# The up projection of a ConvFFN: sums of weight blocks formed by accumulating DMA transfers

## The chip, the cores and the metric

The kernel runs on one core of a Trainium2 chip. The metric is the device time of one execution in microseconds (us); lower is better. Three runs of the kernel before gave 2246.61, 2250.70 and 2250.82 us, with a median of 2250.7. The engines are TensorE (PE, matrix products), VectorE (DVE), ScalarE (ACT), GpSimd (POOL) and SyncE (SP, which here only issues DMA transfers). A core has 16 DMA engines, which queues of the issuing engines feed.

## The reference, cut to what matters

The model has two layers, 1024 tokens (`T`) and a width of 1024. Each layer mixes tokens first and then adds a ConvFFN. Only the ConvFFN is touched here, and it is computed twice, once for each layer:

```
def conv_ffn(h, w_up, conv_w, conv_b, w_down):      # h: 1024 x 1024, w_up: 1024 x 5632
    a, b = jnp.split(h @ w_up, 2, axis=-1)          # each 1024 x 2816
    a_pad = jnp.pad(a, ((0, 0), (CONV_WIDTH - 1, 0), (0, 0)))
    a = sum(a_pad[:, j:j + T] * conv_w[j] for j in range(CONV_WIDTH)) + conv_b   # CONV_WIDTH = 3
    return (jax.nn.silu(a) * b) @ w_down            # w_down: 2816 x 1024
...
x = x + conv_ffn(rmsnorm(x, g_ffn[l]), w_up[l], conv_w[l], conv_b[l], w_down[l])
```

All of it is float32. PE multiplies in a rounded form of it (fp32r), so every operand is split into a rounded upper part `hi` and the remainder `lo`, and one product is three matrix multiplications: hi·hi, hi·lo and lo·hi.

## The kernel before, in words

**Tiling of the up projection.** The products are blocked 2 x 2: the inner dimension of 1024 in two halves, the tokens in two halves of 512, and the two outputs `a` and `b`. The 2816 columns of each output are cut in 22 pieces of 128. One piece is a unit (class `Up`), with four weight blocks A11, A12 (of `a`, first and second half of the inner dimension) and A21, A22 (of `b`). A block is 128 partitions by 512 float32 numbers, 256 KB. A scheme of the Strassen and Winograd kind gives the four output blocks from seven block products instead of eight. The left operands of products 1, 2 and 4 are the loaded blocks A11, A12 and A22; those of products 6, 7, 3 and 5 are sums of the blocks. The right operands are made from the normalised tokens once per layer (`blocks1`, L575 and behind), for all units.

**One unit.** A product (`product`, L1053, matmuls at L1058 to L1060) is 12 matmuls of 128 x 512: four slices of 128 by three multiplications. PE runs the products of a unit in the order 1, 6, 2, 7, 5, 4, 3, adding into three banks: `fx` (products 1 and 2), `fy` (6, 7 and 4) and `fw` (5 and 3). Between them DVE adds results up: `q` (L1092) is product 6 plus `s1`, the copy of product 1 that ACT makes at L1082; `t` (L1097) is formed after product 7, which is added into the same bank as product 6. PE may start product 7 only when DVE has read the bank for `q`. Behind these come the three taps of the convolution (ACT L1117, DVE L1119 and L1123), Silu on ACT (L1138), the products with `b` on DVE (L1107, L1143), and sums of neighbouring units (L1147, `mixed`), which are stored to memory for the down projection (SP, L1170).

**The weights of a unit.** SP loads the four blocks (`load`, L1019) into two tiles of 128 x 1024. `direct` splits A11 (key 1) and the pair A12, A22 (keys 2 and 4): ACT rounds the upper part (L1022) and DVE subtracts it (L1023). Then `sums` (L1042 to L1045) overwrites the blocks in the same two tiles with the four sums, by four tensor_tensor operations, on DVE for the first four units of a layer and on POOL for the other 18:

```
(a0, b0), (a1, b1) = ((t[:, hs(0)], t[:, hs(1)]) for t in self.raw)
tt = (nc.vector if self.soon else nc.gpsimd).tensor_tensor
tt(b1, b0, b1, ALU.add)          # L1042
tt(b0, a0, b0, ALU.subtract)     # L1043
tt(a0, b1, a0, ALU.subtract)     # L1044
tt(a1, a1, a0, ALU.subtract)     # L1045
```

`split67` and `split35` then split two sums each, as one operation of 1024 columns on ACT and one on DVE.

**The order.** The first two units (the pair) run side by side while the right operands are still made. Products 1 and 2 of the next four units (`pre`) are computed in that stage as well, stored, and read back later (`again`, L1075 and L1076); these units are called early here. After the pair, units are run one behind another (`run`), a unit and an early one by turns, and then the remaining twelve. The program names two orders by hand: `follow(..., "order")` puts a split behind a given instruction on ACT and on DVE, and `mix` does so for the sums of neighbours. Everything else is put in order by a scheduler, engine by engine; on its engine each instruction then runs in order. In the profiled execution the up projection of layer 0 lies at about 412 to 841 us and that of layer 1 at about 1595 to 2025 us; the down projections follow.

Of the kernel before, what the change touches and what calls it, by code (L numbers as in the profile page):

```python
# [14 lines left out]
P = 128  # L15
# [4 lines left out]
NF = 22  # L20
# [14 lines left out]
def kernel(  # L35
# [543 lines left out]
    def blocks1(norm, gc, B):  # L579
        rs = norm.done()  # L580
        yield "norm"
        lo, hi = xs[:4], xs[4:]
        a, b = hs(0), hs(1)
        tt = nc.vector.tensor_tensor

        for r in (7, 6, 5, 4, 3):
            B[r] = []
        for j in range(4):
            scaled_x(1, rs, gc, (j, 4 + j))
            nc.sync.dma_start(h_d[j], hi[j][:, b])  # L590
            tt(lo[j][:, b], hi[j][:, b], lo[j][:, b], ALU.subtract)
            tt(lo[j][:, a], lo[j][:, b], lo[j][:, a], ALU.add)
            B[6].append(rl(lo[j][:, a], s="B"))
        for j in range(4):
            B[7].append(rl(lo[j][:, b], s="B"))
        yield "67"
        for j in range(4):
            tt(lo[j][:, b], hi[j][:, b], lo[j][:, a], ALU.subtract)
# [380 lines left out]
    def ffn(l, blocks_, after):  # L979
# [8 lines left out]
        def slot(what, n, make):  # L988
            if what not in ring:
                ring[what] = [make() for _ in range(n)]  # L990
                turn[what] = 0
            turn[what] += 1
            return ring[what][turn[what] % n]

        turn = {}

        def either(n):
            if "A" not in ring:
                ring["A"] = [(V(F32R, "Ah"), V(F32R, "Al")) for _ in range(2)]
            return ring["A"][n]  # L1000

        def raws():
            return [wp.tile([P, 1024], F32, tag="raw", name=nm("wu"), bufs=4) for _ in range(2)]

        class Up:
# [5 lines left out]
            def load(self, k=None):  # L1011
                if k is None:
                    self.load(0)
                    k = 1
                if k == 0:
                    self.raw = slot("raw", 2, raws)
                t = self.raw[k]
                for j in (1, 0) if self.early else (0, 1):
                    nc.sync.dma_start(t[:, hs(j)], w_up[l, j * NF + self.i, :, hs(k)])  # L1019
# [9 lines left out]

            def direct(self):  # L1030
                t = slot("one", 2, lambda: wrl("A"))
                hi, lo = t[:, hs(0)], t[:, hs(1)]
                if self.early:
                    self.split((4,), self.raw[1][:, hs(1)], hi, lo)
                else:
                    self.split((1,), self.raw[0][:, hs(0)], hi, lo)
                    self.split((2, 4), self.raw[1], *slot("two", 2, lambda: (wrl("Ah"), wrl("Al"))))

            def sums(self):
                (a0, b0), (a1, b1) = ((t[:, hs(0)], t[:, hs(1)]) for t in self.raw)  # L1040
                tt = (nc.vector if self.soon else nc.gpsimd).tensor_tensor
                tt(b1, b0, b1, ALU.add)  # L1042
                tt(b0, a0, b0, ALU.subtract)  # L1043
                tt(a0, b1, a0, ALU.subtract)  # L1044
                tt(a1, a1, a0, ALU.subtract)  # L1045
# [142 lines left out]
        def ahead(then, after):  # L1188
            if after is not None:
                after.load(1)  # L1190
            if then is not None and then.early:
                then.again()

        def run(u, last, then, after):
            nxt = [then] if then is not None else []
            if u.s1 is None:
                u.p1()
            u.p6()
            if after is not None:
                after.load(0)  # L1200
            if u.early:
# [3 lines left out]
                u.split35((then.kept, u.opened))  # L1205
                ahead(then, after)
                u.p7()
                u.taps0()
            else:
                u.p2()  # L1210
                each(last[:1], "end")
                u.split35((u.kept, u.opened))
                ahead(then, after)
# [15 lines left out]
            mix(u.ended)  # L1229
            u.p3()  # L1230
# [8 lines left out]
        for n, u in enumerate(seq):  # L1239
            u.n, u.mate = n // 2, seq[n - 1] if n % 2 else None  # L1240
            u.soon = n < 4
        each(pair, "load", "direct")
# [4 lines left out]
        each(pair, "sums")  # L1247
# [3 lines left out]
        each(pair, "split67", "p6", "p7")  # L1251
        next(rest)
        each(pair, "act0", "split35", "p5")
# [6 lines left out]
        then.sums()  # L1260
        each(pair, "p3")
        then.split67()
# [112 lines left out]
        def add_x(ps, k, half):  # L1375
            xv = xs[k][:, hs(half)]
            tt(xv, ps, xv, ALU.add)
# [40 lines left out]
        def down():  # L1418
# [40 lines left out]
            for t0, w in segs_:  # L1459
                c = slice(t0, t0 + w)  # L1460
                for m in range(4):
# [3 lines left out]
                    tt(xv, bank[m][:, c], xv, ALU.add)  # L1465
# [557 lines left out]
```

## Time and profile before

| | |
|---|---|
| median of three runs | 2250.7 us |
| the profiled execution | 2249.9 us |
| its span | 2248.1 us |
| mean granted TensorE clock | 0.997 |
| PE busy | 2207.3 us, 98% of the span |
| DVE busy | 1723.6 us, 77% |
| ACT busy | 1116.3 us, 50% |
| POOL busy | 420.0 us, 19% |
| queue q1 (SP's transfers) | 263.11 MB, 35.4% of the 16 DMA engines |
| queue q0 (POOL's transfers) | 11.65 MB, 1.5% |

The span is the stretch that the hardware profiler recorded; the execution's own time has 1.8 us more. Busy shares are means over the whole span. What holds PE up in one stage is seen only where the trace is cut into stretches of time, and in the waits: an entry such as `[1.75 <-DVE q L1092]` behind an instruction says that its engine stood idle for 1.75 us before it and that DVE's instruction of line 1092, which writes `q`, released it. In a row of a stretch, each engine has its busy time and its number of instructions, followed by the granted clock, the busy share of the DMA engines and the GB/s.

### The profile page before, as it was taken

The page shows a single profiled execution, that of the slowest core. Times are in us where ns is not written, and L with a number is a line of the kernel's source. Part 1 is how long each engine was busy: PE and PEld are TensorE (multiplying, and loading weights), DVE is VectorE, ACT ScalarE, POOL GpSimd, SP SyncE. Part 2 cuts the span into 40 slices and gives each one's busy share as a digit, 9 for nine tenths or more (in the row PEclk, how much of TensorE's full clock was granted, in tenths as well). Part 3 has the DMA queues.
Part 4 walks back from the last instruction along what each step waited for, and adds up shares of the span by engine and source line. Part 5 has one row for each costly group of instructions (what it writes and reads, how often), then busy time and mean ns, then how long its engine had stood idle before and what let it go on. Part 6 is the DMA issues. An engine that isn't in the chain of part 4 may idle for free.

```text
span 2248.1 us, 32203 instructions
## 1 busy us (share of the span) xinstructions
PE 2207.3 (98%) x11522; PEld 1839.3 (82%) x11522; DVE 1723.6 (77%) x3037; ACT 1116.3 (50%) x2085; POOL 420.0 (19%) x409
## 2 busy tenths in 40 slices
PE   9999999999999999999999999999999999999998
PEld 7888887777888888888888888888778888888886
DVE  6886886887877768887756778866987877768877
ACT  6564464543333335456545688874543333335445
POOL 1312210013332210000103323320013322210000
PEclk9999999999999999999999999999999999999999
DMA  6332246334332329544421111036434333329533
GB/s 228 103 104 87 79 156 215 132 127 134 129 122 99 108 78 353 169 136 141 129 85 42 48 48 36 9 116 212 138 127 132 127 122 103 106 74 349 164 94 112
DMA packets 138942, 285.20 MB, mean 127 GB/s; under 512 B 15709, under 2 KB 22446, under 8 KB 138782
## 3 DMA queue, kind: packets, MB, share of 16 engines
q1 hardware_dynamic: 130430, 263.11, 35.4%
q0 software_dynamic: 3600, 11.65, 1.5%
q10 hardware_dynamic: 4752, 8.39, 1.0%
q8 instruction: 90, 1.47, 0.3%
q14 instruction: 70, 0.57, 0.1%
HBM read 211.27 MB, written 71.83 MB: 126 GB/s over the span
## 4 chain that ended last, share of the span: by engine, by line
PE 79%; DVE 11%; ACT 4%; DMA 3%; issue 2%; SPq 0%; POOL 0%; DVEq 0%; ACTq 0%; POOLq 0%
PE dn L1413 6%; PE dn L1414 6%; PE dn L1412 6%; PE fy L1058 5%; PE fy L1060 5%; PE fy L1059 5%; PE fx L1058 3%; PE fx L1059 3%; PE fx L1060 3%; PE fw L1060 3%; PE fw L1058 3%; PE fw L1059 3%; PE op L195 2%; PE op L196 2%; PE op L194 2%
## 5 line engine op out<-in xcount | busy, mean ns | idle before, releaser
L1412 PE MATMUL dn<-db,da 128*128 128x512 f32 (+1 forms) x628 | 242.5, 386 | 0.0
L1413 PE MATMUL dn<-db,da 128*128 128x512 f32 (+1 forms) x628 | 242.1, 386 | 0.3 <-DVE db L1342 0.3
L1414 PE MATMUL dn<-db,da 128*128 128x512 f32 (+1 forms) x628 | 241.6, 385 | 0.0
L1058 PE MATMUL fy<-B,Ah 128*128 128x512 f32 x496 | 195.4, 394 | 8.5 <-DVE q L1092 7.3
L1060 PE MATMUL fy<-B,Al 128*128 128x512 f32 x496 | 194.0, 391 | 0.4 <-DVE Al L1023 0.4
L1059 PE MATMUL fy<-B,Ah 128*128 128x512 f32 x496 | 193.8, 391 | 0.0
L1042 POOL TENSOR_TENSOR wu<-wu,wu 128x512 f32<-128x512 f32 x36 | 47.2, 1311 | 730.7 <-DVE Al L1023 568.5
L1022 ACT ACTIVATE Ah<-wu 128x1024 fp32r<-128x1024 f32 x124 | 130.4, 1052 | 102.9 <-PE fy L1059 60.3
L1023 DVE TENSOR_TENSOR Al<-wu,Ah 128x1024 fp32r<-128x1024 f32 x124 | 160.8, 1298 | 8.5 <-ACT Ah L1022 7.4
L1413 PEld LDWEIGHTS dn<-db,da 128*128 128x128 f32 x628 | 117.9, 188 | 25.6 <-DVE db L1342 1.8
L1412 PEld LDWEIGHTS dn<-db,da 128*128 128x128 f32 x628 | 118.0, 188 | 24.1 <-issue 0.2
L1060 PE MATMUL fw<-B,Al 128*128 128x512 f32 x352 | 137.7, 391 | 0.0
L1059 PE MATMUL fw<-B,Ah 128*128 128x512 f32 x352 | 137.0, 389 | 0.0
L1058 PE MATMUL fw<-B,Ah 128*128 128x512 f32 x352 | 137.0, 389 | 0.0
L1414 PEld LDWEIGHTS dn<-db,da 128*128 128x128 f32 x628 | 117.9, 188 | 23.2
L1342 DVE TENSOR_TENSOR db<-bl,db 128x512 fp32r<-128x512 f32 x154 | 105.8, 687 | 27.9 <-ACT db L1341 27.3
L1058 PEld LDWEIGHTS fy<-B,Ah 128*128 128x128 f32 x496 | 93.5, 188 | 33.7 <-DVE q L1092 12.3
L1341 ACT ACTIVATE db<-bl 128x512 fp32r<-128x512 f32 x154 | 95.7, 621 | 34.0 <-PE dn L1414 26.4
L1060 PEld LDWEIGHTS fy<-B,Al 128*128 128x128 f32 x496 | 93.5, 189 | 20.9 <-DVE Al L1023 1.1
L1059 PEld LDWEIGHTS fy<-B,Ah 128*128 128x128 f32 x496 | 93.5, 188 | 19.0
L1138 ACT ACTIVATE fc<-fc 128x512 f32<-128x512 f32 x88 | 54.9, 626 | 106.3 <-DVE fc L1119 85.3
L1341 ACT ACTIVATE da<-wb 128x512 fp32r<-128x512 f32 x88 | 55.1, 629 | 99.4 <-PE dn L1413 67.4
(415 smaller groups left out, 6152.2 us busy)
## 6 DMA issues: line engine op xcount, KB each, us to landing
wu<-in_w_up_dram SPq DMA_DIRECT2D x176, 256.0 KB, 3.0
bl<-gb_d SPq DMA_DIRECT2D x154, 256.0 KB, 2.8
gb_d<-fc SPq DMA_DIRECT2D x132, 256.0 KB, 2.5
wb<-in_w_down_dram SPq DMA_DIRECT2D x44, 256.0 KB, 3.9
wa<-in_w_down_dram SPq DMA_DIRECT2D x22, 512.0 KB, 7.8
wo<-in_a_wo_dram SPq DMA_DIRECT2D x16, 512.0 KB, 3.8
xre<-om_d SPq DMA_DIRECT2D x32, 256.0 KB, 4.2
x_r<-x SPq DMA_DIRECT2D x32, 256.0 KB, 2.4
```

What stands on the lines that cost most here:

```text
L1022: a = nc.scalar.activation(hi, src, AF.Copy)
L1023: b = nc.vector.tensor_tensor(lo, src, f(hi), ALU.subtract)
L1042: tt(b1, b0, b1, ALU.add)
L1058: mm(ps, wr, hr, start=(first and j == 0), stop=False, skip_group_check=True)
L1059: mm(ps, wr, hl, start=False, stop=False, skip_group_check=True)
L1060: mm(ps, wl, hr, start=False, stop=(stop and j == 3), skip_group_check=True)
L1138: silu[0] = nc.scalar.activation(self.c[half], self.c[half], AF.Silu)
L1341: nc.scalar.activation(w[:, hs(0)], t, AF.Copy)
L1342: b = tt(w[:, hs(1)], t, f(w)[:, hs(0)], ALU.subtract)
L1412: mm(o, hi, bh, start=first, stop=False, skip_group_check=True)
L1413: mm(o, hi, bl, start=False, stop=False, skip_group_check=True)
L1414: mm(o, lo, bh, start=False, stop=stop or n == NP - 1, skip_group_check=True)
```

## The change

**Where the sums are made.** The four sums of a unit are no longer made by DVE or POOL. SP loads A11 and A22 into one tile `R`, A12 into a half tile `Q` and A11 once more into a half tile `T`. POOL then issues DMA transfers that read a weight block from memory and add it to what stands in the target (`more`, with `accum_op=ALU.add`): T += A21 and T += A22 give the sum for product 6; R += A21 on both halves gives those for products 7 and 5 (after `direct` has split A11 and A22 from the same tile); T += A12 gives that for product 3 (after product 6's sum was split). These are five accumulating transfers of 256 KB per unit, 110 per layer. The left operand of product 3 is thus formed in the same place as that of product 6, from it.

**Splits.** The keys split together change: (1, 4) as one operation of 1024 columns, 2 alone, (7, 5) together, 6 alone, 3 alone. `split3` is placed by hand behind product 5's sum (`u.summed`) on DVE and behind Silu on ACT. The splits go to tiles named by what is dead there (`area`), six of one kind and four of another, instead of rings of two; the four raw tiles are now R0, R1 (by turns), Q and T (a half for each parity of the unit).

**Signs.** An accumulating transfer can only add here, so some sums come out with another sign. On the right side three kinds of sum (one addition and two subtractions) become a scalar_tensor_tensor that computes -p - q in place of a tensor_tensor (`neg_sub`, 12 per layer), and in the down projection the result is subtracted from x instead of added.

The core of the diff:

```diff
@@ blocks1
+        def neg_sub(o, p, q):
+            nc.vector.scalar_tensor_tensor(o, p, -1.0, q, ALU.mult, ALU.subtract)
+
...
-            tt(lo[j][:, a], lo[j][:, b], lo[j][:, a], ALU.add)
+            neg_sub(lo[j][:, a], lo[j][:, b], lo[j][:, a])
...
-            tt(lo[j][:, b], hi[j][:, b], lo[j][:, a], ALU.subtract)
-            tt(hi[j][:, a], hi[j][:, a], lo[j][:, a], ALU.subtract)
+            neg_sub(lo[j][:, b], hi[j][:, b], lo[j][:, a])
+            neg_sub(hi[j][:, a], lo[j][:, a], hi[j][:, a])
@@ class Up
+            def load(self):
+                self.load_r()
+                self.load_q()
+                self.sum_t(0)
+                self.sum_t(1)
+
+            def load_r(self):
+                self.place()
+                nc.sync.dma_start(self.R[:, hs(0)], self.block(0, 0))
+                nc.sync.dma_start(self.R[:, hs(1)], self.block(1, 1))
+
+            def load_q(self):
+                if not self.early:
+                    nc.sync.dma_start(self.Q, self.block(0, 1))
+                nc.sync.dma_start(self.T, self.block(0, 0))
+
+            def more(self, t, j, k):
+                nc.gpsimd.dma_start(t, self.block(j, k), accum_op=ALU.add)
+
+            def sum_t(self, k):
+                self.more(self.T, 1, k)
+
+            def sum_r(self):
+                for h in range(2):
+                    self.more(self.R[:, hs(h)], 1, 0)
+
+            def sum_s4(self):
+                self.more(self.T, 0, 1)
...
-            def sums(self):
-                (a0, b0), (a1, b1) = ((t[:, hs(0)], t[:, hs(1)]) for t in self.raw)
-                tt = (nc.vector if self.soon else nc.gpsimd).tensor_tensor
-                tt(b1, b0, b1, ALU.add)
-                tt(b0, a0, b0, ALU.subtract)
-                tt(a0, b1, a0, ALU.subtract)
-                tt(a1, a1, a0, ALU.subtract)
-
-            def split67(self, past=None):
-                self.split((6, 7), self.raw[0], *either(self.i == 1), past)
-
-            def split35(self, past=None):
-                self.split((3, 5), self.raw[1], *either(self.i != 0), past)
+                    self.split((1, 4), self.R, hi, lo)
+                    self.one(2, self.Q, "Z3" if self.pos == 1 else "Z2")
+
+            def split75(self, past=None):
+                hi, lo = (area(k) for k in (("Z2", "Z3") if self.pos == 1 else ("Y0", "Y1")))
+                self.split((7, 5), self.R, hi, lo, past)
+
+            def split6(self, past=None):
+                self.one(6, self.T, "Z7" if self.pos % 2 else "Z6", past)
+
+            def split3(self, past=None):
+                self.one(3, self.T, ("Z6", "Z7")[self.pos] if self.pos < 2 else "Z3", past)
@@ run(u, last, then, after)
             u.act0()
-            each(nxt, "sums")
+            each(nxt, "sum_r")
             u.p5()
             mix(u.summed)
+            u.split3((u.acted, u.summed))
+            each(two, "load_q")
             for v in nxt:
-                v.split67((u.acted, u.drained))
+                v.split6((u.acted, u.drained))
+                v.sum_s4()
+            for v in two:
+                v.sum_t(0)
+                v.sum_t(1)
...
             u.p4()
             mix(u.ended)
+            each(nxt, "split75")
             u.p3()
@@ the tail of the down projection (and add_x alike)
-                    tt(xv, bank[m][:, c], xv, ALU.add)
+                    tt(xv, xv, bank[m][:, c], ALU.subtract)
```

**How it moves POOL's instructions.** The first place is on POOL, among the late units of layer 0 (`wu_639` to `wu_642` are the four raw tiles; after the change 639 and 642 are R0 and R1, 640 is Q and 641 is T). Before, for two units:

```order
L1042 TENSOR_TENSOR wu_640_3520<-wu_639_3519,wu_640_3520 128x512
L1043 TENSOR_TENSOR wu_639_3519<-wu_639_3519 128x512
L1044 TENSOR_TENSOR wu_639_3519<-wu_640_3520,wu_639_3519 128x512
L1045 TENSOR_TENSOR wu_640_3520<-wu_640_3520,wu_639_3519 128x512
L1042 TENSOR_TENSOR wu_642_3522<-wu_641_3521,wu_642_3522 128x512
L1043 TENSOR_TENSOR wu_641_3521<-wu_641_3521 128x512
L1044 TENSOR_TENSOR wu_641_3521<-wu_642_3522,wu_641_3521 128x512
L1045 TENSOR_TENSOR wu_642_3522<-wu_642_3522,wu_641_3521 128x512
```

Now, for two units:

```order
L1038 DMA wu_639_3519<-in_w_up_dram 128x512 x2
L1038 DMA wu_641_3521<-in_w_up_dram 128x512
L1038 DMA wu_642_3528<-in_w_up_dram 128x512
L1038 DMA wu_641_3521<-in_w_up_dram 128x512
L1038 DMA wu_642_3528<-in_w_up_dram 128x512
L1038 DMA wu_641_3521<-in_w_up_dram 128x512 x4
```

Eight tensor operations became ten issues of transfers, of which those on R and on T stand in one in-order queue, one behind another.

**How it moves DVE's instructions.** The second place is on DVE ahead of `q` of the third unit behind the pair, in layer 0 (the wait of PE at 520 us before). `Ah` and `A` are halves of splits. Before, with `q` of that unit as the last row:

```order
L1023 TENSOR_TENSOR Al_693_3823<-wu_641_3521,Ah_692_3822 128x1024
L1107 TENSOR_TENSOR fc_740_4259<-fc_740_4259,s1_727_4110 128x512
L1023 TENSOR_TENSOR A_643_3531<-wu_640_3520,A_643_3531 128x512
L1112 TENSOR_TENSOR q_734_4208<-fw_741_4268,q_734_4208 128x512
L1023 TENSOR_TENSOR A_644_3532<-wu_641_3521,A_644_3532 128x512
L1092 TENSOR_TENSOR q_744_4330<-fy_743_4317,s1_736_4229 128x512
```

Now:

```order
L1134 TENSOR_TENSOR s1_727_4116<-fy_733_4208,s1_727_4116 128x512
L1052 TENSOR_TENSOR Ah_693_3823<-wu_639_3519,Ah_692_3822 128x1024
L1052 TENSOR_TENSOR A_648_3540<-wu_641_3521,A_648_3540 128x512
L1052 TENSOR_TENSOR Ah_694_3824<-wu_641_3521,Ah_694_3824 128x512
L1135 TENSOR_TENSOR fc_740_4268<-fc_740_4268,s1_727_4116 128x512
L1052 TENSOR_TENSOR A_646_3538<-wu_642_3528,A_645_3537 128x512
L1052 TENSOR_TENSOR A_647_3539<-wu_640_3520,A_647_3539 128x512
L1140 TENSOR_TENSOR q_734_4221<-fw_741_4275,q_734_4221 128x512
L1120 TENSOR_TENSOR q_744_4345<-fy_743_4332,s1_736_4242 128x512
```

Five splits stand ahead of this `q` (now L1120), where three stood before; the first reads R0 and the next two read T, all behind accumulating transfers; the last two read R1 and Q as SP loaded them. (Lines of the changed kernel: loads L1029 to L1035, accumulating transfers L1038, splits L1051 on ACT and L1052 on DVE, products L1086 to L1088.)

More of the change, by code (lines that the diff above doesn't have):

```diff
@@ L986, in ffn, with area, raws @@
         ring = {}
-        def slot(what, n, make):
+        def area(what):
+            if not ring:
+                for k in "X0 X1 X2 X3 Z2 Z3".split():
+                    ring[k] = wrl("A")
             if what not in ring:
[L990 to L1003, printed above, removed]
+                for k in "Y0 Y1 Z6 Z7".split():
+                    ring[k] = V(F32R, "Ah")
+            return ring[what]
+        def raws(what):
+            if what not in ring2:
+                ring2[what] = wp.tile([P, 1024], F32, tag="raw", name=nm("wu"), bufs=4)
+            return ring2[what]
+        ring2 = {}
         class Up:
@@ L1009, in __init__, with block, place @@
                 self.s1 = None
[L1011 to L1019, printed above, removed]
+            def block(self, j, k):
+                return w_up[l, j * NF + self.i, :, hs(k)]
+            def place(self):
+                n = self.pos % 2
+                self.R = raws(f"R{n}")
+                self.Q, self.T = (raws(k)[:, hs(n)] for k in "QT")
+            def load(self):
[20 more added lines that the diff above has]
+                self.more(self.T, 0, 1)
             def split(self, keys, src, hi, lo, past=None):
@@ L1186, in mix @@
                     mixing.pop(0)
[L1188 to L1192, printed above, removed]
         def run(u, last, then, after):
             nxt = [then] if then is not None else []
+            two = [after] if after is not None else []
             if u.s1 is None:
@@ L1198, in run @@
             u.p6()
-            if after is not None:
-                after.load(0)
+            each(two, "load_r")
             if u.early:
@@ L1204, in run @@
                 each(last, "end")
-                u.split35((then.kept, u.opened))
-                ahead(then, after)
                 u.p7()
@@ L1211, in run @@
                 each(last[:1], "end")
-                u.split35((u.kept, u.opened))
-                ahead(then, after)
+                if then is not None and then.early:
+                    then.again()
                 u.p7()
@@ L1239, in ffn @@
         for n, u in enumerate(seq):
-            u.n, u.mate = n // 2, seq[n - 1] if n % 2 else None
-            u.soon = n < 4
-        each(pair, "load", "direct")
+            u.pos, u.n, u.mate = n, n // 2, seq[n - 1] if n % 2 else None
+        each(pair, "load", "direct", "sum_r")
         each(pair, "p1")
@@ L1246, in ffn @@
         pair[1].p2()
-        each(pair, "sums")
         for u in us[2:PRE]:
@@ L1250, in ffn @@
         next(rest)
-        each(pair, "split67", "p6", "p7")
+        each(pair, "split6", "split75", "sum_s4", "p6", "p7")
         next(rest)
-        each(pair, "act0", "split35", "p5")
+        each(pair, "act0", "split3", "p5")
         next(rest)
@@ L1259, in ffn @@
         then.direct()
-        then.sums()
+        then.sum_r()
         each(pair, "p3")
-        then.split67()
+        then.split6()
+        then.sum_s4()
+        then.split75()
         last = pair
@@ L1376, in add_x @@
             xv = xs[k][:, hs(half)]
-            tt(xv, ps, xv, ALU.add)
+            tt(xv, xv, ps, ALU.subtract)
         s1 = [None] * 4
```

10 lines of the change are left out of this document (5 added, 5 removed).

## The prediction

> **What bounds the kernel now.** I read the shares of the engines first, then the waits of PE, then the two up stages cut into stretches, and last the single instructions at each wait.
>
> ```profile
> PE 2207.3 (98%) x11522; PEld 1839.3 (82%) x11522; DVE 1723.6 (77%) x3037; ACT 1116.3 (50%) x2085; POOL 420.0 (19%) x409
> PE fy L1058 <- DVE q L1092: 7.3, 6, 2.6
> ```
>
> PE is busy for 98% of the span, and the change leaves its matmuls as they are. So a gain can only come from the time in which PE stands, and a loss only from new standing. The second row (microseconds in total, times, longest) is the largest wait of PE in the whole program, and it lies in the touched code: product 7 waits until DVE has read product 6 for `q`. The stretches show where in the stages PE stands (length, then busy time of PE, weight loads, DVE, ACT and POOL, then granted clock, DMA share, GB/s):
>
> ```profile
> 405.00:450.00 45.00, 43.04 (x183) 33.64 (x183) 40.83 (x59) 25.13 (x40) 0.00 (x0) 1.00 0.32 113
> 500.00:550.00 50.00, 46.90 (x204) 37.86 (x203) 40.60 (x58) 18.74 (x27) 11.94 (x9) 1.00 0.40 134
> 600.00:650.00 50.00, 49.30 (x217) 40.20 (x216) 41.60 (x58) 19.82 (x28) 15.35 (x10) 1.00 0.35 118
> 650.00:825.00 175.00, 175.00 (x774) 144.96 (x773) 124.56 (x172) 59.40 (x88) 50.42 (x36) 1.00 0.28 96
> 1675.00:1725.00 50.00, 47.34 (x200) 37.97 (x199) 41.30 (x59) 16.40 (x24) 16.10 (x11) 0.97 0.42 138
> 1825.00:2000.00 175.00, 175.00 (x774) 144.91 (x773) 126.25 (x175) 62.41 (x92) 50.40 (x36) 1.00 0.28 94
> ```
>
> In the late units (650 to 825 and 1825 to 2000 us) PE never stands, so nothing can be gained there, whatever POOL does. DVE is busy there for 71 to 72%; at the early units for 81 to 91%. PE stands for 2.0, 3.1, 0.7 and 2.7 us in the other four stretches. The late rows also give the pitch of a matmul: 175 / 774 = 0.226 us, or 2.7 us for a product of 12.
>
> The single waits, and the matmuls behind the longest:
>
> ```profile
> 502.38 0.50 PE L1058 MATMUL fy<-B,Ah 128*128 128x512 f32 x1 [1.75 <-DVE q L1092]
> 520.39 0.50 PE L1058 MATMUL fy<-B,Ah 128*128 128x512 f32 x1 [1.35 <-DVE q L1092]
> 620.91 0.50 PE L1058 MATMUL fy<-B,Ah 128*128 128x512 f32 x1 [0.70 <-DVE q L1092]
> 1664.30 0.50 PE L1058 MATMUL fy<-B,Ah 128*128 128x512 f32 x1 [0.28 <-DVE q L1092]
> 1683.53 0.62 PE L1058 MATMUL fy<-B,Ah 128*128 128x512 f32 x1 [2.58 <-DVE q L1092]
> 1687.28 0.40 PE L1058 MATMUL fy<-B,Ah 128*128 128x512 f32 x1
> 1802.36 0.50 PE L1058 MATMUL fy<-B,Ah 128*128 128x512 f32 x1 [0.69 <-DVE q L1092]
> ```
>
> They add to 7.35 us. Behind the wait of 2.58 us, nine matmuls take from 1683.53 to 1687.28, 3.75 us instead of 9 x 0.226 = 2.03: another 1.72 us, in the only stretch with a clock of 0.97. So the six waits cost 9.07 us.
>
> **Why q is late.** At the first large wait the rows of DVE and of POOL, side by side:
>
> ```profile
> 490.13 1.62 POOL L1042 TENSOR_TENSOR wu<-wu,wu 128x512 f32<-128x512 f32 x1 [143.91 <-DVE Al L1023]
> 495.75 1.75 POOL L1045 TENSOR_TENSOR wu<-wu,wu 128x512 f32<-128x512 f32 x1
> 491.11 1.72 DVE L1023 TENSOR_TENSOR Al<-wu,Ah 128x1024 fp32r<-128x1024 f32 x1
> 492.75 1.77 DVE L1119 SCALAR_TENSOR_TENSOR fc<-q,cs,fc 128x511 f32<-128x511 f32 x1
> 494.45 1.24 DVE L1123 SCALAR_TENSOR_TENSOR fc<-edge,cs,fc 128x1 f32<-128x1 f32 x1
> 496.28 1.25 DVE L1123 SCALAR_TENSOR_TENSOR fc<-edge,cs,fc 128x2 f32<-128x2 f32 x1
> 501.65 0.68 DVE L1092 TENSOR_TENSOR q<-fy,s 128x512 f32<-128x512 f32 x1
> 503.04 0.74 DVE L1119 SCALAR_TENSOR_TENSOR fc<-q,cs,fc 128x510 f32<-128x510 f32 x1
> 503.70 0.21 DVE L1123 SCALAR_TENSOR_TENSOR fc<-edge,cs,fc 128x2 f32<-128x2 f32 x1
> 503.83 1.22 DVE L1023 TENSOR_TENSOR Al<-wu,Ah 128x1024 fp32r<-128x1024 f32 x1
> ```
>
> From 490.13 to 497.50 POOL makes its first four sums, and four DVE instructions in this time take 5.98 us; the same kinds take 1.22 + 0.74 + 2 x 0.21 = 2.38 once POOL rests. That is 3.6 us, and DVE then works through a backlog without a gap up to `q`, which is 1.75 us late. The same stands at 1672 us, ahead of the wait of 2.58. Two waits (4.33 us, and the 1.72 of slow clock) are thus the price of POOL's sums, which the change takes away.
>
> The other four (3.02 us) have another reason:
>
> ```profile
> 517.35 0.63 ACT L1022 ACTIVATE A<-wu 128x512 fp32r<-128x512 f32 x1 [1.69 <-DMA wu<-in_w_up_dram]
> 518.02 1.72 DVE L1023 TENSOR_TENSOR A<-wu,A 128x512 fp32r<-128x512 f32 x1 [2.34 <-ACT A L1022]
> 519.66 0.68 DVE L1092 TENSOR_TENSOR q<-fy,s 128x512 f32<-128x512 f32 x1
> ```
>
> A split stands ahead of `q` in DVE's order, its upper part waits on ACT for a load, and so DVE stands for 2.34 us. At 518 POOL's sums also stretch the split by 1.0 us (1.72 against 0.68 for a 512-wide one). The new order still has splits of loaded blocks at this place. So I credit the wait at 520 with its stretch of 1.0, and of what is left, 2.0 us, one half: 1.0 stays as a cost.
>
> **The cost of the change, part by part.**
>
> *POOL's tensor operations* (144) vanish and nothing in the up stages waits for POOL's time itself. *The 32 sums of DVE* in the first stages (16 per layer at 0.69) vanish too, where DVE is at 91%: a gain in the stretch from 405 us that I leave at nothing, as PE's gaps there hang on the norm.
>
> *Signs.*
>
> ```profile
> L566 DVE SCALAR_TENSOR_TENSOR x<-x,cs,rs 128x512 f32<-128x512 f32 x16 | 11.6, 749 | 0.1
> L598 DVE TENSOR_TENSOR x<-x,x 128x512 f32<-128x512 f32 x4 | 2.8, 690 | 0.0
> ```
>
> The nearest row to the new operation, two operands in SBUF, takes 749 ns, against 690: 12 x 0.06 = 0.7 us of DVE per layer, of which nine (0.5) stand ahead of the first product 6. There the split for it has half its former width (0.6 us less on DVE), so I put it at nothing; uncovered it would be 1.0 for both layers. The subtraction in the down projection is one tensor_tensor as before.
>
> In the Trainium skill, "Vector Engine (DVE) Microarchitecture Reference" (section 7, Points that are easy to get wrong) says that a scalar_tensor_tensor with two SBUF sources that are not bf16 runs at half the throughput. By that each would take some 1.4 us, the nine 6.2 us per layer, and the sum would end near 2256; the row above, of just such an operation, speaks against it.
>
> *The accumulating transfers.* None is in the trace, so their time from issue to landing, L, is the unknown. Rows (KB each, median us to landing; and POOL's time for an issue, 547 ns):
>
> ```profile
> wu<-in_w_up_dram SPq DMA_DIRECT2D x176, 256.0 KB, 3.0
> xre<-in_x_dram POOLq DMA_DIRECT2D x8, 256.0 KB, 4.6
> L318 POOL DMA_DIRECT2D xre<-in_x_dram x8 | 4.3, 547 | 0.0
> ```
>
> Below, L is 3.0, a plain load of the same blocks by SP; above, 9.2, two passes of the slowest of POOL's 256 KB transfers, one to read and one to add. I take 4.6, the row of POOL's own queue from memory, since what is added is on the way anyhow. They are 220 x 256 KB = 57.7 MB; 28.8 MB in some 430 us is 67 GB/s, and with 0.28 for 96 GB/s that is 20 points more of the DMA engines, on 28 to 42%. No queue is full by that.
>
> Where the sums are waited for, from the changed order:
>
> 1. At the start of the units behind the pair. T comes free when product 3's split of the first unit is done; I take the place where the split of key 3 ends now, 459.5. Product 6 of the next unit begins at 478.68.
>
> ```profile
> 458.33 1.22 DVE L1023 TENSOR_TENSOR Al<-wu,Ah 128x1024 fp32r<-128x1024 f32 x1
> 478.68 0.39 PE L1058 MATMUL fy<-B,Ah 128*128 128x512 f32 x1
> ```
>
> In these 19.2 us must fit the load (3.0), two sums one behind another (2 x (0.55 + L)) and the split (0.63 + 0.69): 14.6 with L = 4.6, so it is hidden up to L = 6.9. In the late units products 4 and 3, a whole unit of seven and product 1 lie between, ten products or 27 us: hidden up to L = 10.8.
>
> 2. At the third unit behind the pair (the second place of the order shown above). Behind `direct`'s lower part stand two issues (1.1) and L, then on ACT the split of keys 7 and 5, Silu, a tap, Silu and the upper part of product 3's split, with three DVE instructions between, then its lower part on DVE, for which product 3 of the unit before waits. With the rows
>
> ```profile
> 456.89 1.06 ACT L1022 ACTIVATE Ah<-wu 128x1024 fp32r<-128x1024 f32 x1
> L1138 ACT ACTIVATE fc<-fc 128x512 f32<-128x512 f32 x88 | 54.9, 626 | 106.3 <-DVE fc L1119 85.3
> ```
>
> it is 1.1 + 4.6 + 1.06 + 4 x 0.63 + (2 x 0.74 + 0.68) + 0.68 = 12.1, and with a little for hand-overs 12.3. In that time PE has 53 matmuls, 12.0 us. So PE waits for 0.3 here, once per layer: 0.6. It grows with L, microsecond by microsecond. If product 3 stands, `q` of the next unit and product 7 shift with it, no more. At the later units `direct` stands a product or two earlier, and there it is hidden.
>
> *The split of product 3 alone* adds an ACT and a DVE instruction per unit (0.63 and 0.69, against 0.5 each for the half of a wide one): 0.1 to 0.2 us per unit of 18.9 us, under DVE's 28% of idle time late; PE has no cover to lose there.
>
> *The sum.* 9.07 gained, 1.0 of load waits and 0.6 of the new wait back: 7.5. From 2249.9 of the profiled execution to 2242.4; the median of the runs lies 0.8 above it, so 2243.2; I say 2243.4.
>
> **The rivals.**
>
> (a) *The sums land late.* At L = 9.2 the third unit's wait is 4.6 + 0.3 and the start's 2 x (9.2 - 6.9) = 4.6, in both layers 19.0 against 8.1 of the rest: 2261.6. It decides from L = 7.4, where 2 x 3.1 + 4 x 0.5 = 8.2 has eaten the gain; over 2255 it comes at L = 8.2. For it speaks that an addition has to read and write its target; against it that 128 x 2 KB rows are on 16 engines that are two thirds idle.
>
> (b) *The waits move.* ACT and DVE run in order, and now stand behind transfers at more places (a split of T and two of R per unit). If each of the six waits comes back in another form, nothing is left of the gain: 2249 to 2251. The four waits for loads speak for it; the late units' idle DVE against.
>
> (c) *All goes well*: L = 3.0 and no load late: 2249.9 - 9.07 - a few tenths of DVE's 16 sums, and 0.8: 2241, at best 2239.
>
> (d) *Each accumulation reads twice.* Then L is twice a plain load, 6.0, hidden at the start, 0.3 + 1.4 at the third unit, 3.4 in both layers: 2246.0. In the Trainium skill, "Collectives: The Full Stack" (Part 3, The bandwidth ceiling) says that an add by DMA needs two source reads, hence two descriptors per chunk and half the rate; no run so far shows it here.
>
> (e) That the sums don't leave POOL isn't possible: its order shows the transfers in their place.
>
> **How the numbers follow.** The forecast (2241.5 to 2245.5) has 0.40, (c) 0.10, (d) 0.13 (2245 to 2248), (b) 0.18, (a) 0.17, and the half rate of scalar_tensor_tensor 0.02. Less than 0.2% (4.5 us) can't be told from no change here. So faster (under 2246.2) is 0.40 + 0.10 + half of (d), 0.57; same takes (b) and the other half, 0.25; slower 0.18 from (a) and the rest. The range leaves out the upper part of (a) and the best of (c): 2239 to 2256. The likeliest case's own is 2241.5 to 2245.5.
>
> **What would show it right or wrong.** Right: in the waits of PE the row of `q` falls from 7.3 to 2 or less, the clock is 1.00 from 1675 to 1725, the edge taps take 0.21 at all places, the accumulating transfers land in 4 to 6 us. Signs: the new operation takes some 0.75. Wrong: PE's waits name the split of product 3 or 6, with ACT waiting for transfers into `wu`; or the late stretches lose their 100%; or L is over 7.4. A time under 2239 would mean that DVE's relief at the pair stage counted.

## The result, and the profile after

The changed kernel takes 2275.1 us (median of four runs, 2271.22 to 2278.66), beside 2250.8 us of the kernel before on the same chip: 1.0105 of it, with a 95% interval of 1.0087 to 1.0122. The forecast was 2243.4 with a range of 2239 to 2256. The change is 24 us slower, and the range does not hold it.

The profiled execution took 2276.55 us with a span of 2274.8, 26.7 longer than before. Where they lie shows in the first starts of the stages. The view of one line's matmuls gives for each shape its shortest, median and longest time, and the first and last start. Before, for the up projection and the two down projections:

```profile
L1058 PE MATMUL fx<-B,A x144: 389/389/389, 411.8 to 2005.8; 128*128 128x512 f32 x144
L1412 PE MATMUL dn<-db,da x308: 387/389/476, 841.4 to 1053.2; 128*128 128x512 f32 x154
L1412 PE MATMUL dn<-db,da x320: 278/389/791, 2022.8 to 2234.9; 128*128 128x512 f32 x148, 128*128 128x256 f32 x12
```

After:

```profile
L1086 PE MATMUL fx<-B,A x288: 387/389/791, 414.9 to 2037.9; 128*128 128x512 f32 x144
L1439 PE MATMUL dn<-db,da x308: 387/389/628, 858.4 to 1072.7; 128*128 128x512 f32 x154
L1439 PE MATMUL dn<-db,da x320: 278/389/791, 2049.5 to 2261.5; 128*128 128x512 f32 x148, 128*128 128x256 f32 x12
```

Layer 0's up stage grew from 429.6 (841.4 - 411.8) to 443.5 us, by 13.9. In layer 1, whose first such matmul starts at 1593.6 before and 1612.6 after, it grew from 429.2 to 436.9, by 7.7. That is 21.6 us. The other 5.1 lie ahead of the first up stage and between the two; this part moves by some 4 us from one execution to another with nothing changed there (in two of the experiments below, whose orders are the same up to this place, one and the same matmul of the first stage starts at 449.18 and at 445.12).

The page of the changed kernel, the waits of PE, and the same stretches of the early units (busy time of PE, weight loads, DVE, ACT, POOL; clock, DMA share, GB/s):

```profile
PE 2215.3 (97%) x11522; PEld 1845.4 (81%) x11522; DVE 1654.5 (73%) x3049; ACT 1118.7 (49%) x2129; POOL 396.2 (17%) x485
q0 software_dynamic: 35280, 69.33, 16.6%
PE fw L1086 <- ACT A L1051: 18.1, 6, 6.0
L1086 PE MATMUL fy<-B,Ah 128*128 128x512 f32 x344 | 135.4, 394 | 0.8 <-DVE q L1120 0.8
500.00:550.00 50.00, 43.16 (x177) 33.77 (x176) 31.53 (x49) 13.39 (x23) 11.14 (x13) 0.93 0.72 171
550.00:600.00 50.00, 45.96 (x193) 36.59 (x192) 34.41 (x56) 16.72 (x28) 11.98 (x14) 0.97 0.85 199
650.00:700.00 50.00, 50.00 (x223) 41.38 (x222) 32.63 (x53) 17.64 (x30) 11.11 (x13) 1.00 0.78 186
1700.00:1750.00 50.00, 44.34 (x183) 34.83 (x182) 32.35 (x53) 14.76 (x24) 12.16 (x14) 0.93 0.75 182
```

Three things are to be seen. The wait for `q` fell from 7.3 to 0.8 us, as forecast, and DVE has less to do. In its place PE waits for 18.1 us, six times, at product 3 (bank `fw`, left operand `A`) for ACT's part of that product's split. And the matmuls behind these waits are slow again: 177 of them from 500 to 550 us take 43.16 us, 0.244 each instead of 0.226, with a clock of 0.93. The three stretches that hold the long waits lose 3.2, 2.3 and 3.0 us by that (busy time less 0.226 for each matmul). And PE waits for `s`, ACT's copy of product 1, for 5.4 us instead of 1.4, at the start of the two stages. The late units are at 100% as before.

The price of the transfers, in the changed kernel (KB each, median us to landing; then POOL's group with its busy time and the mean ns of one record; records of issues in a row overlap, so the price of an issue is the busy time over 220, 0.86 us):

```profile
wu<-in_w_up_dram POOLq DMA_DIRECT2D x220, 256.0 KB, 6.2
wu<-in_w_up_dram SPq DMA_DIRECT2D x168, 256.0 KB, 3.7
L1038 POOL DMA_DIRECT2D wu<-in_w_up_dram x220 | 189.5, 950 | 812.4 <-DMA wu<-in_w_up_dram 371.6 <-DVE Ah L1052 370.4 <-DVE A L1052 31.7
```

The first of the six waits, from the timelines of DVE, POOL, ACT and PE:

```profile
505.20 1.22 DVE L1052 TENSOR_TENSOR A<-wu,A 128x1024 fp32r<-128x1024 f32 x1
509.69 2.60 POOL L1038 DMA_DIRECT2D wu<-in_w_up_dram  x3 [3.98 <-ACT s L1110]
517.97 1.06 ACT L1051 ACTIVATE Ah<-wu 128x1024 fp32r<-128x1024 f32 x1 [7.57 <-DMA wu<-in_w_up_dram]
522.92 0.61 ACT L1051 ACTIVATE A<-wu 128x512 fp32r<-128x512 f32 x1
523.59 0.80 PE L1086 MATMUL fw<-B,A 128*128 128x512 f32 x1 [5.99 <-ACT A L1051]
```

The split that frees R of the third unit ends at 506.42 on DVE. POOL issues three transfers from 509.69 on, the first of which belongs to R of the fourth unit, whose load SP had issued at 503.71. (The entry of POOL's wait names ACT's `s`, which ended at the same time; the load landed at 509.13, and POOL issues behind it.) The two for the third unit go out at about 510.6 and 511.4 and have landed at 517.97, when ACT can split keys 7 and 5. Behind that stand, in ACT's order, Silu, a tap, a split of another unit, Silu, and at 522.92 the upper part of product 3's split. T, which this split reads, had been ready for long: product 3 waits for a sum that it does not use.

### The profile page after: what moved, and what is told of

Same layout as the page of the kernel before. It is cut to its first block, busy times and chain, and to the rows that moved or that the text cites. A ratio compares the mean times of both kernels' runs of the same rounds, so it can differ in the third digit from the quotient of the medians.

```text
span 2274.8 us, 32670 instructions
## 1 busy us (share of the span) xinstructions
PE 2215.3 (97%) x11522; PEld 1845.4 (81%) x11522; DVE 1654.5 (73%) x3049; ACT 1118.7 (49%) x2129; POOL 396.2 (17%) x485
## 5 line engine op out<-in xcount | busy, mean ns | idle before, releaser
L1038 POOL DMA_DIRECT2D wu<-in_w_up_dram x220 | 189.5, 950 | 812.4 <-DMA wu<-in_w_up_dram 371.6
L1051 ACT ACTIVATE A<-wu 128x512 fp32r<-128x512 f32 (+1 forms) x122 | 92.3, 758 | 186.3 <-PE fx L1087 137.7
L1052 DVE TENSOR_TENSOR A<-wu,A 128x512 fp32r<-128x512 f32 (+1 forms) x122 | 103.7, 851 | 67.6 <-ACT A L1051 64.8
L1086 PE MATMUL fy<-B,Ah 128*128 128x512 f32 x344 | 135.4, 394 | 0.8 <-DVE q L1120 0.8
L1088 PE MATMUL fy<-B,Ah 128*128 128x512 f32 x344 | 134.1, 390 | 1.8 <-DVE Ah L1052 1.8
L1087 PE MATMUL fy<-B,Ah 128*128 128x512 f32 x344 | 134.5, 391 | 0.0
L1086 PE MATMUL fx<-B,A 128*128 128x512 f32 x288 | 113.2, 393 | 2.0 <-ACT s L1110 2.0
L1088 PE MATMUL fx<-B,A 128*128 128x512 f32 x288 | 112.5, 391 | 0.7 <-DVE A L1052 0.7
L1087 PE MATMUL fx<-B,A 128*128 128x512 f32 x288 | 112.1, 389 | 0.0
L1051 ACT ACTIVATE Ah<-wu 128x512 fp32r<-128x512 f32 (+1 forms) x90 | 71.1, 821 | 77.6 <-DMA wu<-in_w_up_dram 71.9
L1110 ACT ACTIVATE s<-fx 128x512 f32<-128x512 f32 x44 | 26.0, 596 | 163.9 <-PE fx L1088 163.9
L1052 DVE TENSOR_TENSOR Ah<-wu,Ah 128x512 fp32r<-128x512 f32 (+1 forms) x90 | 83.9, 935 | 30.8 <-ACT Ah L1051 30.8
L194 PE MATMUL op<-om,wor 128*128 128x512 f32 x256 | 101.6, 398 | 1.8 <-ACT om L230 1.8
```

The lines of the kernel that those rows point to most:

```text
L194: mm(ps, wr[:, k, :], hr, start=(k == 0), stop=False)
L1038: nc.gpsimd.dma_start(t, self.block(j, k), accum_op=ALU.add)
L1051: a = nc.scalar.activation(hi, src, AF.Copy)
L1052: b = nc.vector.tensor_tensor(lo, src, f(hi), ALU.subtract)
L1086: mm(ps, wr, hr, start=(first and j == 0), stop=False, skip_group_check=True)
L1087: mm(ps, wr, hl, start=False, stop=False, skip_group_check=True)
```

## The experiments

Theory A was that each wait is an in-order engine that stands behind an instruction which waits for a sum. Theory C was that adding in a transfer is dear by itself. Their rival B was that the sums as such come too late for the products that need them. Each ratio below is to runs of the kernel before on the same chip, beside those of the experiment.

**Product 3's split ahead of the split of R.** One row changes place on ACT at four units per layer, with what follows from it (the line that matters; `u.three` is product 3's split on ACT and on DVE):

```diff
-            each(nxt, "split75")
+            for v in nxt: v.split75(u.three)
```

> Edit: the split of keys 7 and 5 of the next unit is put by hand behind product 3's split of the unit before, on ACT and on DVE. On ACT that swaps the two at the four units behind the pair and an early one, in both layers; the sums and their transfers stay. Theory A (product 3 waits only because its split stands in ACT's order behind the split of R, which waits for accumulating transfers): the six waits of product 3 (18.1 us) fall under 3 us, and with them the slow matmuls behind them (about 7 us); 2250 to 2256. Rival B (the sums as such land too late, whatever the order): the wait comes back at product 7, which needs the split of R, or at product 6, and the time stays at 2268 or more.

Measured: 2258.2 us, 1.0033 of before (1.0021 to 1.0045), by the ratios 16 us less than the changed kernel. The waits of product 3 for ACT are gone; product 7, which needs the split of R, waits nowhere. What came instead is in the waits of PE:

```profile
PE fw L1086 <- DVE t L1130: 5.1, 2, 3.2
```

It misses the 2250 to 2256 of theory A by 2 us, for a second wait of the same kind that I had not seen, and it is far from B.

**POOL's order.** In each layer two transfers into R change place in POOL's order, and nothing on another engine (the lines that matter):

```diff
-                    self.more(self.R[:, hs(h)], 1, 0)
+                    sums_r.append(self.more(self.R[:, hs(h)], 1, 0))
+                    if len(sums_r) > 1: follow(sums_r[-1], sums_r[-2], 'order')
```

> Edit: the two sums into R of a unit are issued behind those of the unit before it, also where R of the later unit needs no split first (the early units). It moves ten rows in POOL's order and none on any other engine. In the changed kernel the third unit's sums stood behind one for the fourth unit's R, whose load had just been issued (3.3 us between the split that frees R and POOL's first issue). Theory A with POOL's queue as a second cause: the two longest waits of product 3 (5.99 and 5.21 us) fall by about 3 to 4 us each, the shorter four stay; 2263 to 2269. If POOL's order does not matter: 2272 or more.

Measured: 2266.05 us, 1.0066 (1.0049 to 1.0083), by the ratios 9 us less than the changed kernel:

```profile
PE fw L1086 <- ACT A L1051: 11.0, 6, 2.7
```

All six waits fell from 18.1 to 11.0, and the two at the third unit from 5.99 and 5.21 to 2.33 and 2.67. So there half of the wait or more was one transfer, for another unit's R, standing ahead in POOL's queue.

**Both.**

> Edit: both of the above. Theory A: as the first, since product 3 then waits for nothing that POOL's order could delay; 2249 to 2255. If the two add: 6 us or more below the first.

Measured: 2256.35 us, 1.0023 (1.0011 to 1.0035), a microsecond above the expected 2249 to 2255 and not to be told from the first experiment. The wait for `t` is still there, 7.4 us. From the timelines of POOL, ACT, DVE and PE of this kernel:

```profile
520.77 1.72 POOL L1038 DMA_DIRECT2D wu<-in_w_up_dram  x2 [1.66 <-DMA wu<-in_w_up_dram]
528.11 0.85 POOL L1038 DMA_DIRECT2D wu<-in_w_up_dram  x1 [5.62 <-DMA wu<-in_w_up_dram]
533.19 0.63 ACT L1051 ACTIVATE Ah<-wu 128x512 fp32r<-128x512 f32 x1 [6.04 <-DMA wu<-in_w_up_dram]
533.85 0.69 DVE L1052 TENSOR_TENSOR Ah<-wu,Ah 128x512 fp32r<-128x512 f32 x1 [5.98 <-ACT Ah L1051]
534.46 0.68 DVE L1130 TENSOR_TENSOR t<-fw,t 128x512 f32<-128x512 f32 x1
535.29 0.76 PE L1086 MATMUL fw<-B,A 128*128 128x512 f32 x1 [4.28 <-DVE t L1130]
```

T of the fourth unit takes two sums one behind another. The first is issued at about 521 and has landed at 528.11, the second at 533.19; then ACT and DVE split it for product 6. On DVE this split stands ahead of `t` of the unit before. `t` reads the bank that product 3 writes next, so product 3 waits for the fourth unit's sums. It is the same pattern once more, on another engine.

**The split of product 6 behind t.** One row on DVE per layer, with the two edits above:

```diff
-                v.split6((u.acted, u.drained))
+                v.split6((u.acted, u.summed))
```

> Edit: both edits of the third run, and the split for product 6 of the next unit is put by hand behind product 5's sum t instead of behind t's first step. That moves one row of DVE's order, at the fourth unit behind the pair, in each layer; PE, ACT and POOL keep their order. In the third run product 3 of the third unit waited for t (4.28 and 3.09 us), since on DVE the split for the fourth unit stood ahead of t and waited for two accumulating transfers into T one behind another. Theory A (each wait is an in-order engine standing behind an instruction that waits for a sum): both waits go, with some 3 us of slow matmuls; a wait of 1 us or less may stand at product 6 of the fourth unit; 2246 to 2250. Rival B (T's two sums are late as such): product 6 of the fourth unit waits for as long instead, and the time stays at 2255 or more.

Measured: 2250.9 us, 1.0006 (0.9996 to 1.0016): level with the kernel before, a microsecond above what was expected. The stretches of the early units in this kernel (columns as above):

```profile
500.00:550.00 50.00, 49.60 (x215) 39.37 (x214) 37.05 (x60) 18.05 (x29) 13.48 (x16) 1.00 0.84 208
1690.00:1740.00 50.00, 49.56 (x216) 39.93 (x216) 38.72 (x63) 19.14 (x32) 12.20 (x14) 1.00 0.83 206
```

PE stands for 0.4 us in each, while the same 220 accumulating transfers run at the same 6.2 us to landing. That is against B: the sums come in time for the products that use them. At the price of these additions, what made the change slow is where three instructions wait for them. With the order mended the change gives back its loss, but gains nothing over the kernel before.

**A copy in place of the addition** (the addition is left out; every engine's order stays):

```diff
-                nc.gpsimd.dma_start(t, self.block(j, k), accum_op=ALU.add)
+                nc.gpsimd.dma_start(t, self.block(j, k))
```

> Edit: POOL's 220 transfers copy instead of adding (the addition is left out, so the operands of products 6, 7, 5 and 3 are single blocks); every engine's order is the same. Theory C (an accumulating transfer keeps the DMA engines busy for twice as long as a copy of the same bytes, and that makes sums and loads late): the share of POOL's queue falls from 16.6 to about 9%, its time to landing from 6.2 to about 4, the waits of product 3 from 18.1 to about 9 us; 2258 to 2266. If the adding costs nothing beside a copy: share, landing and time as in the changed kernel, 2272 or more.

Measured: 2249.4 us, 0.9994 (0.9982 to 1.0005), well under the expected 2258 to 2266.

```profile
q0 software_dynamic: 21200, 69.33, 9.8%
wu<-in_w_up_dram POOLq DMA_DIRECT2D x220, 256.0 KB, 4.6
L1038 POOL DMA_DIRECT2D wu<-in_w_up_dram x220 | 117.9, 538 | 858.3 <-DVE Ah L1052 402.4 <-DMA wu<-in_w_up_dram 321.6 <-DVE x L544 51.9
PE fw L1086 <- ACT A L1051: 4.2, 2, 2.4
```

With the same bytes in the same places, the copy takes 8.3 points of the DMA engines where the addition takes 15.1 (each less the 1.5 of before), lands in 4.6 us instead of 6.2 and costs POOL 0.54 us an issue instead of 0.86. Theory C stands: in the time of the DMA engines an accumulating transfer is 1.8 copies, in landing 1.35. The packets (17600 here, 31680 with the addition, each less the 3600 of before) differ in size and not in bytes: in the packet records a copy is 64 of 4 KB and an addition 128 of 2 KB, each with 16 short ones. The loss needed both, the dear transfers and the order: copies in the old order give 0.9994, additions in the mended order 1.0006. At 4.6 us, the value that the prediction took, the four shorter waits are gone and the two at the third unit are 1.81 and 2.37 us.

**The copy with POOL's order mended.**

> Edit: the copies of the fourth run (the addition left out) with POOL's order of the second. In the fourth run 4.6 us to landing left waits of 1.81 and 2.37 us at product 3, once per layer. If POOL's order is their second cause (theory A), they go, and with them 3.9 us of slow matmuls: 2241 to 2245, which is what the prediction gave for a landing of 4.6 us. If the chain from the split of R to product 3 is itself longer than its cover, they stay: 2248 to 2250.

Measured: 2245.95 us, 0.9972 (0.9963 to 0.9981), 3.5 us less than the copy alone and a microsecond above the expected bracket. The waits of product 3 are 0.32 and 1.55 us. In layer 0 that is the 0.3 of the prediction's sum; in layer 1 there is 1.2 more, so the agreement in layer 0 is in part luck.

**The kernel before without POOL's sums** (the 18 later units of a layer use blocks that are not summed):

```diff
-                tt = (nc.vector if self.soon else nc.gpsimd).tensor_tensor
+                if not self.soon:
+                    return
+                tt = nc.vector.tensor_tensor
```

> Edit to the kernel before: POOL's sums are left out (the 18 later units of a layer use unsummed blocks). It measures the gain that the prediction started from. If POOL's sums stretch DVE (theory): the waits of 1.75 and 2.58 us at q and the slow matmuls behind the second go, the one of 1.35 falls by 1.0; 7 us less than before, 2243 to 2246. If the waits at q come from loads alone: 2249 or more.

Measured: 2242.7 us, 0.9968 (0.9955 to 0.9981). That is 7.8 us less than the 2250.5 beside it (4 to 10 by the interval), a little more than expected; the waits for `q` are 1.2 us in all, the longest 0.7. What POOL's sums cost the kernel before was read rightly, as far as this interval tells.

**Sums moved from POOL to DVE, in the kernel before.** If POOL's sums cost so much by stretching DVE, DVE may as well make them. Nothing else changes:

```diff
-            u.soon = n < 4
+            u.soon = n < 6        # and 5, 8, True (all 22)
```

> Edit to the kernel before: DVE makes the sums of two more units per layer (the first two that POOL made). If the stretch is what counts: DVE pays 8 x 0.6 = 4.8 us for two units and is spared 3.6 us and more of stretch at the first; the large waits shrink only if the first of POOL's sums then falls where DVE has slack: 2246 to 2251. If DVE's load at this place is what counts, the waits grow: 2252 to 2256.

> Edit to the kernel before: DVE makes the sums of one more unit per layer (five instead of four). With the sums of two more units on DVE the time was 0.9984 of before and the two longest waits at q were gone: POOL's first sums then fell behind q. If the first of POOL's sums is what made q late (theory), one unit is enough: 2245 to 2248. If both units' sums have to go, the waits of 1.35 and 0.28 us stay and 2248 to 2251 comes out.

> Edit to the kernel before: DVE makes the sums of four more units per layer (eight instead of four). If POOL's sums at the early units still cost (theory: stretch), the waits of 0.70 and 0.69 us go as well and 2244 to 2247 comes out. If DVE has no slack left for 2.4 us more per unit at the early units, q or t is late again: 2249 or more.

> The kernel before with DVE making the sums of six units, once more and with more rounds, beside the two others: 0.9975 to 0.9990 of before if the first measurement holds; an interval that reaches 1 otherwise.

> Edit to the kernel before: DVE makes the sums of all 22 units of a layer, POOL none. DVE is busy for 71% in the late stretches, and four sums add 2.4 us to a unit of 18.9 us, 13 points. If a sum on DVE costs nothing wherever DVE has slack (theory): the time of eight units on DVE, 2244 to 2248, and as little as without POOL's sums at best. If the order on DVE makes q, t or a split late in the late units too: 2250 or more, with PE no longer at 100% there.

| DVE's units per layer | median, us | ratio to before | interval | wait for q, us |
|---|---|---|---|---|
| 5 | 2248.6 | 0.9984 | 0.9975 to 0.9993 | 1.8 |
| 6 | 2246.6 | 0.9984 | 0.9973 to 0.9994 | 1.7 |
| 6, again | 2247.1 | 0.9982 | 0.9970 to 0.9993 | 1.3 |
| 8 | 2246.0 | 0.9973 | 0.9961 to 0.9984 | 1.6 |
| 22 | 2244.0 | 0.9964 | 0.9953 to 0.9976 | 1.1 |

One unit is enough to take the long waits at `q` away (1.8 us in all instead of 7.3), so it was the first of POOL's sums that made `q` late; more units give little each, with intervals that overlap. With all 22 the time is that of the kernel with no POOL sums at all (0.9968). The late stretch of that kernel:

```profile
650.00:825.00 175.00, 175.00 (x774) 144.90 (x773) 139.41 (x208) 59.44 (x89) 0.00 (x0) 1.00 0.28 97
```

DVE went from 71 to 80% here, and PE is still at 100%. This one-line version is faster than both kernels: 2244.0 us beside 2251.7.

## Why the prediction was wrong

**The gain was right.** The prediction put the waits for `q` at 9.07 us with their slow matmuls, and credited 8.1 of them. The kernel before without POOL's sums gives 7.8, and the changed kernel's wait for `q` fell from 7.3 to 0.8 us. The page of the Trainium skill "SBUF — State Buffer" (Who interferes with whom) says that a DVE operation with two SBUF inputs and a GpSimd operation that reads SBUF exclude each other on a shared pair of ports. The trace agrees: an edge tap of two columns took 1.25 us beside POOL's sums and 0.21 without. With all sums on DVE, PE's late stretch stays at 100%.

**The signs cost nothing**, as I had it by another way: the new operation takes what a tensor_tensor takes. From DVE's groups of the changed kernel, 380 to 650 us:

```profile
L566 DVE SCALAR_TENSOR_TENSOR x<-x,cs,rs 128x512 f32<-128x512 f32 x16 | 11.5, 748 | 0.1
L587 DVE SCALAR_TENSOR_TENSOR x<-x,x 128x512 f32<-128x512 f32 x8 | 5.3, 685 | 0.0
```

At 685 ns there is no halved throughput, so the rule that I weighed from the Trainium skill, "Vector Engine (DVE) Microarchitecture Reference" (section 7), does not hold for this operation.

**The size of L was too small.** I took 4.6 us, the row of POOL's plain transfers, on the ground that what is added is on the way anyhow. A copy from the same queue lands in that (4.6 and 4.8 in the two runs with copies); the addition takes 6.2 in the median. I also took L as one number. It was longer the more was in flight: at the third unit the last of three lands about 6.5 us behind its issue (511.4 to 517.97). At the third of layer 0's waits, two transfers start at 581.04, right behind two others:

```profile
577.58 1.72 POOL L1038 DMA_DIRECT2D wu<-in_w_up_dram  x2 [4.89 <-DVE Ah L1052]
581.04 1.72 POOL L1038 DMA_DIRECT2D wu<-in_w_up_dram  x2 [1.75 <-DVE A L1052]
592.79 1.06 ACT L1051 ACTIVATE Ah<-wu 128x1024 fp32r<-128x1024 f32 x1 [5.05 <-DMA wu<-in_w_up_dram]
594.94 0.50 PE L1086 MATMUL fw<-B,A 128*128 128x512 f32 x1 [2.67 <-ACT A L1051]
```

The second of them, issued at about 581.9, has landed at 592.79, after 10.9 us: above my upper bound of 9.2. In the same way the sum "20 points more of the DMA engines" came from the bytes at the price of a load. The share went from 0.40 to 0.72 in the stretch from 500 us, from 0.28 to 0.78 from 650 to 700, and at the start of the stage, as shown below, to 0.94, so "No queue is full by that" is false there.

**The step that failed most is the second place of the sum**, the new wait of "0.3 here, once per layer: 0.6". The chain was the right one, instruction by instruction: landing, split of keys 7 and 5, Silu, tap, Silu, split of product 3, product 3. Its part behind the landing took 523.59 - 517.97 = 5.6 us, where my terms give 6.4. Its head, from the freeing of R to the landing, took 11.55 us (506.42 to 517.97) where the sum has 1.1 + 4.6 = 5.7. It was wrong in three ways. I priced two issues at 0.55 each and none ahead of them, but POOL's queue held a transfer for the fourth unit, which waited for a load that SP had only just issued: 3.3 us from the freeing of R to the first issue, then some 0.86 for each of the two issues ahead of the last. L was too small: 6.6 from the last issue. And the sentence "at the later units `direct` stands a product or two earlier, and there it is hidden" is false: four more waits of 1.36, 2.67, 1.91 and 0.96 us stand there. I had not counted the matmuls at those units as I had at the third, where the cover was 11.2 us (506.42 to 517.60) and not 12.0. Together 18.1 us of waiting stand where 0.6 was forecast, and the slow matmuls behind them, which I had counted on the side of the gain, I left out on the side of the cost. The sign of being wrong that the prediction named first is what PE's waits show.

**A wait that the sum did not have.** At the start of the stages, where the prediction has no term for a cost, PE waits for `s`. Before and after (the stretch, SP's 512 KB loads of `wa`, the weights that `pre` uses, and the wait):

```profile
400.00:415.00 15.00, 15.00 (x67) 12.41 (x67) 12.59 (x18) 8.78 (x12) 0.00 (x0) 1.00 0.56 185
wa<-in_w_up_dram SPq DMA_DIRECT2D x8, 512.0 KB, 4.1
PE fx L1058 <- ACT s L1082: 1.4, 2, 0.7
400.00:415.00 15.00, 15.00 (x68) 12.43 (x67) 9.37 (x13) 6.56 (x10) 5.06 (x6) 1.00 0.94 233
wa<-in_w_up_dram SPq DMA_DIRECT2D x8, 512.0 KB, 7.5
PE fx L1086 <- ACT s L1110: 5.4, 6, 1.6
419.93 1.06 ACT L1051 ACTIVATE Ah<-wa 128x1024 fp32r<-128x1024 f32 x1 [3.39 <-DMA wa<-in_w_up_dram]
421.42 1.06 ACT L1110 ACTIVATE s<-fx 128x512 f32<-128x512 f32 x2
422.05 0.50 PE L1086 MATMUL fx<-B,A 128*128 128x512 f32 x1 [1.01 <-ACT s L1110]
```

On ACT `s` stands behind a split of `wa`, whose plain load is now late: six accumulating transfers are issued in this stretch, and the DMA engines are at 0.94. That is 4 us more of waiting in all. It is read from the timeline; no experiment changes this place alone. With copies in the old order the load lands in 5.0 us and the wait is 2.9.

**A second wait was hidden behind the first.** The prediction held the start and the late units to be the tight places for T. T of the fourth unit, which comes free late and needs two sums, was tight as well: in the third experiment PE waited 7.4 us for it by way of DVE's order.

**The rivals.** Rival (a) had the right sign, at 0.17, but its price of 2261.6 us at L = 9.2 rests on two places per layer, of which the first shows no wait, and falls short of 2275 even with L above what was measured in the median. Rival (b), that ACT and DVE run in order and stand behind transfers at more places, at 0.18, names the mechanism that the experiments show, but it held the loss to what was gained, 2249 to 2251. Rival (d), that each accumulation reads twice, has the size about right: in the Trainium skill, "Collectives: The Full Stack" (Part 3, The bandwidth ceiling) names two source reads for the add of a collective, and the runs show 1.8 times the engine time of a copy. By the packet records of the changed kernel from 500 to 700 us, one of 2 KB takes 193 ns on average where it adds and 102 in SP's transfers beside it. What is read twice is not shown: the profile's count of HBM reads rose by 55.6 MB with the addition and with the copy alike. Its L of 6.0 is close to the 6.2 measured, but its time of 2246 fails by the same wrong sum as the forecast.

**What stays open.** By its median the mended order is level with before, and not 8 us faster like the version with all sums on DVE. In the profiled execution its two up stages take 425.9 and 426.6 us, 6.3 less in all than before and 2.4 more than with all sums on DVE; its waits for `s` are 4.7 us there, against 1.4. But that execution, of 2246.9 us, is the fastest of ten with a median of 2250.9, and what makes the others longer is not shown.

## What to carry to other kernels

Before a sum, a load or a transfer is put in place of an operation, list what stands behind its waiters on each in-order engine, and count the cover at every unit, not at the one that looks tightest: here an instruction stood behind one that waited for a sum it did not use, on ACT, on DVE and in POOL's queue in turn. In this kernel an accumulating transfer costs 1.8 copies in the time of the DMA engines and 1.35 in landing time, and what counts for a wait is the longest landing under load (10.9 us) rather than the median (6.2). And where one engine slows another by its mere presence, try first to give its work to the slowed one: four operations of 0.69 us on DVE were cheaper than four of 1.5 on POOL beside it.

## What the runs showed of the hardware that was not expected

- An accumulating transfer of 256 KB from memory to SBUF keeps POOL busy for 0.86 us at its issue, a copy for 0.54, and lands in 6.2 us (copy 4.6), up to 10.9 with four in flight.
- Beside accumulating transfers plain ones land later: SP's 512 KB loads of `wa` took 7.5 us in the median instead of 4.1.
- A scalar_tensor_tensor with a constant and two SBUF operands takes 685 ns for 512 columns, less than the 748 of one with a column of scalars (L566).
- Behind a wait of PE the matmuls can run at a pitch of 0.41 to 0.45 us, about half speed, for seven to ten of them, at once (5.99 us of waiting) or 1.7 us later (2.67 us). The length of the wait alone does not decide it: it followed waits of 1.81 (copies) and 1.82 us (POOL's order), but not those of 1.75, 1.86 and 1.91, nor one of 2.67 (POOL's order, at 1707.55 us). What decides is not settled here.
